# A hybrid diffusion block on one core: ScalarE evicts each time-mixer projection twice, makes the key factor and copies the decays

## The chip, the core and the metric

The kernel runs on one core of a Trainium2 chip. The metric is device time in microseconds; three timed runs of the kernel before gave 1555.4, 1558.96 and 1561.5 us. Engines are named as in the profile: PE multiplies matrices, DVE is VectorE, ACT is ScalarE, POOL is GpSimd, SP issues the transfers. Each engine runs its own instructions strictly in the order in which they stand in the program; semaphores make one wait for another.

## The reference, cut to what matters

Two layers over 1024 latent tokens and a prefix of 256 context tokens, model width 1024. The first (even) layer mixes by pooling and a short convolution. The second (odd) layer mixes by a bidirectional RWKV-7 scan over 512 channels in 8 heads, beside a Conformer convolution. The change lies in what prepares that scan:

```python
def token_shift_mix(z, mu):
    zp = jnp.pad(z, ((0, 0), (1, 1), (0, 0)))
    nb = 0.5 * (zp[:, :-2] + zp[:, 2:])
    return z + (nb - z) * mu
...
    r = token_shift_mix(r, mu[0])
    k = token_shift_mix(k, mu[1])
    v = token_shift_mix(v, mu[2])
...
    for d in range(2):
        logw = -jax.nn.softplus(-(w0[d] + jnp.tanh(uw @ w1[d]) @ w2[d])) - 0.5
        decay = jnp.exp(-jnp.exp(logw.astype(jnp.float32)))
        a = jax.nn.sigmoid(a0[d] + (ua @ a1[d]) @ a2[d])
        k_d = heads(k * (1.0 + (a - 1.0) * k_a)).astype(jnp.float32)
```

The shift is computed as (1 - mu) z + (mu / 2)(left neighbour + right neighbour): one array scaled by `omu` = 1 - mu, a sum of two neighbours, and a multiply-add with `hmu` = mu / 2. The key factor 1 + (a - 1) k_a is written with tanh: a = (1 + tanh) / 2, so that it is `ta` times one value of each channel plus another (`ka`).

## The kernel before

Channels lie on the 128 partitions, tokens along the free axis: 1024 latent tokens and 256 of the context, `TT` = 1280. The program has three parts in time: the even layer to about 609 us, the preparation of the odd layer (`odd_in`) to about 940 us, and the scan, with the Conformer branch beside it, to the end.

In `odd_in` the 512 channels are four blocks `j` of 128. For each block the job `dense` projects three arrays, keys, values and receptances (i = 0, 1, 2), with 24 matmuls for each stretch of 512 or 256 tokens (`project`, `L992`: every product of weights and activations is split into high and low parts, hence three for each of eight depths). Each stretch comes out of PSUM by a copy on ACT (`L1009`) into `Z`, an array with a column of zeros at each border. Two sets of three such arrays take turns. The weights of a projection are split by a cast on ACT (`L972`) and a subtraction on POOL (`L974`).

The job `shift` then makes the token shift: POOL adds the two neighbours into `both` (`L1061`), DVE scales `Z` in place (`L1063`) and adds the scaled `both` (`L1066`). `keys` normalises the shifted keys (`L1093` to `L1128`, on ACT, PE and DVE).

Each block then has five preparations `prep(j, u)`, one for each 256 tokens (u = 4 is the context, which comes first). One preparation, in its order of dependence: two matmuls and a tanh on ACT give `thw` (`L1149`, `L1153`); two more give `ta` (`L1160`, `L1166`); DVE adds 1 and runs two scans over `thw`, forward and backward (`L1171` to `L1173`); ACT makes the exponentials F and E of it (`L1178`, `L1180`). DVE makes the key factor `kd` from `ta` (`L1187`) and POOL multiplies it by the keys (`L1191`). DVE makes `bk` in two halves from `ta` and F (`L1194`, `L1198`, `L1199`), and the other part of it from POOL's product (`L1220`). POOL copies the decays at the ends of the 64-token chunks out of E into `PT` (`L1211`, `L1212`), multiplies receptances by E (`L1216`, into `ar`) and, for latent tokens, adds the two directions of `kd` (`L1232`, into `kb`). DVE makes the rest of `ar` (`L1223`, `L1224`) and, for latent tokens, the bonus (`L1236`, and after a matmul `L1243`). PE transposes `bk` (`L1299`), ACT and DVE copy it out of PSUM (`L1306`, `L1309`), SP stores everything. Most of these arrays (`thw`, `ta`, `E`, `F`, `kd`, `bk`, `ar`, `kb`) have one buffer each.

Four more projections (`NZ`), for the gate of the mixer, follow at the end (`L1025`, `L1027`, `L1037`).

The order of the instructions on each engine is not written out. Every job is a generator that says what it is about to issue: `yield "D", 460` is a DVE instruction with a planned cost, "A" is ACT, "G" POOL, "P" PE, "S" SP; "E" waits for a noted event, "J" for another job, "R" takes a buffer from a list (`RES2`) that `free` gives back. `Lists.run` picks the next instruction of the engine that would be free first, by priority and planned start, while the program is built; the chip then follows that order. A changed cost or engine so changes the order of the whole stage. The scan has a plan of its own.

Of the kernel before, what the change touches and what calls it, by code (L numbers as in the profile page):

```python
# [8 lines left out]
F32 = mybir.dt.float32  # L9
F32R = mybir.dt.float32r  # L10
AF = mybir.ActivationFunctionType
ALU = mybir.AluOpType
# [3 lines left out]
D = 1024  # L16
T = 1024
TC = 256
TT = T + TC
# [77 lines left out]
class Lists:  # L97
# [13 lines left out]
    def spawn(self, gen, prio):  # L111
        e = Job(gen, prio, self.cur.ready if self.cur else 0.0)
        self.advance(e)
        self.jobs.append(e)
        return e
# [6 lines left out]
    def note(self, key):  # L122
        self.ev[key] = self.cur.ready

    def free(self, name, what=None):
        self.res[name].append((self.cur.ready, what))
# [53 lines left out]
class Kern:  # L180
# [14 lines left out]
               wr=[0.0], w00=[0.0], w10=[0.0], w01=[], w11=[])  # L195
    KP = 7
    RES2 = dict(psd=[0.0] * 3, pm=[0.0], pw=[0.0] * 2, pt=[0.0], ss=[0.0], sq=[0.0], ta=[0.0], EF=[0.0], kd=[0.0], bk=[0.0], ar=[0.0],
                kb=[0.0], Vx=[0.0], X=[0.0], thw=[0.0], kkm=[0.0] * 2, ex=[0.0] * 4, LB=[0.0] * 2, gt=[0.0] * 2, wr=[], w0=[], w1=[],
                **{f"z{q}{i}": [0.0] for q in range(2) for i in range(3)})
    OP = (((0, 1), 512), ((0, 1, 4, 5, 6, 7), 0), ((4, 5, 6, 7), 512))  # L200
    NZ = 4
# [3 lines left out]
    LB = (256, 512, 0, 768)  # L205
# [678 lines left out]
    def odd_in(self, es):  # L884
        tc, nc, A = self.tc, self.nc, self.A
        cp, dr, hn = self.co, self.dr, self.hn
        hmu, omu, hw0, ka = self.hmu, self.omu, self.hw0, self.ka
# [11 lines left out]
        def rhs(src, k, b, c0, n):  # L899
            return hn[src, k, b][:, c0:c0 + n]  # L900
# [43 lines left out]
        zp = es.enter_context(tc.tile_pool(name="zp", bufs=1))  # L944

        ZS = [[zp.tile([128, TT + 3 if i < 2 else T + 2], F32, name=f"Z{q}{i}") for i in range(3)] for q in range(2)]
        for z in ZS[0] + ZS[1]:
            for c in (0, T + 1, TT + 2):
                if c < z.shape[1]:
                    nc.gpsimd.memset(z[:, c:c + 1], 0.0)  # L950
        SEG = (((1, 0, T), (T + 2, T, TC)),) * 2 + (((1, 0, T),),)

        L = Lists(self.SL, self.LAT, self.RES2)
        spawn, note, free = L.spawn, L.note, L.free
# [24 lines left out]
        def project(blocks, eat):  # L979
            i = used[0]  # L980
            used[0] += 1
            yield "E", ("w", i)
            w = self.ready[i]
            js = []
            for s, c0, m in blocks:
                yield "R", "psd"
                ps = self.psd.tile([128, 512], F32, tag="d", name="d")[:, :m]
                seq = [(k, a, b) for k in range(KD) for a, b in ((1, 0), (0, 1), (0, 0))]
                for q, (k, a, b) in enumerate(seq):
                    if q % 3 == 0:  # L990
                        yield "P", 3 * m / 2.4
                    nc.tensor.matmul(ps, lhsT=w[a][:, k, :], rhs=rhs(s, k, b, c0, m), start=(q == 0), stop=(q == len(seq) - 1))  # L992
                js.append(spawn(eat(s, c0, m, ps), 4))
            free(f"w{(n - i) % 2}")
            return js

        def dense():
            for j in range(NJ):
                spawn(keys(j), self.KP if j else 4)
                for u in (4, 0, 1, 2, 3):  # L1000
                    spawn(prep(j, u), 6 + (5 * j + (u + 1) % 5) / 100)
                spawn(over(j), 5)
                for i, blks in enumerate((BLK, BLK, XB)):
                    yield "R", f"z{j % 2}{i}"

                    def ev(src, c0, m, ps, j=j, i=i):
                        z = 1 + c0 + (0 if src == "x" else T + 1)
                        yield "A", m * 0.833 + 55
                        nc.scalar.copy(ZS[j % 2][i][:, z:z + m], ps)  # L1009
                        free("psd")  # L1010
                    spawn(shift(j, i, (yield from project(blks, ev))), self.KP if j else 4)
                    if (j, i) == (NJ - 1, 1):
                        self.s_actc.close()
                        ex = es.enter_context(tc.tile_pool(name="ex", bufs=1, side="right"))
            for i in range(self.NZ):
                yield "R", "ex"
                yield "R", "ex"
                z, g = [ex.tile([128, T], F32, tag=f"ex{i % 2}{q}", name="ex") for q in range(2)]
                spawn(gates(i, z, g, (yield from project(XB, ez(z)))), self.ZP)

        def ez(t):
            def f(src, c0, m, ps):
                z = t[:, c0:c0 + m]
                yield "A", 480
                nc.scalar.activation(out=z, in_=ps, func=AF.Tanh, scale=0.5)  # L1025
                yield "D", 605
                nc.vector.scalar_tensor_tensor(out=z, in0=z, scalar=1.0, in1=ps, op0=ALU.add, op1=ALU.mult)  # L1027
                free("psd")
            return f

        def gates(i, z, g, js):
            yield "S", 600, 3700
            nc.sync.dma_start(out=g, in_=self.GD[i])
            for e in js:
                yield "J", e
            yield "D", 1140
            nc.vector.tensor_tensor(out=z, in0=z, in1=g, op=ALU.mult)  # L1037
            yield "S", 600, 2500
            nc.sync.dma_start(out=self.ZCD[i], in_=z)
            free("ex")  # L1040
            free("ex")

        def over(j):

            for u in range(5):
                yield "E", ("prep", j, u)
            for i in range(3):
                free(f"z{j % 2}{i}")
            free("kkm")

        def shift(j, i, js):

            for e in js:
                yield "J", e
            yield "E", "room"
            yield "R", "ss"
            z, mi = ZS[j % 2][i], (1, 2, 0)[i]
            both = sp.tile([128, TT], F32, tag="ss", name="both")
            for p, o, m in SEG[i]:
                yield "G", m * 2.1 + 150  # L1060
                nc.gpsimd.tensor_tensor(out=both[:, o:o + m], in0=z[:, p - 1:p - 1 + m], in1=z[:, p + 1:p + 1 + m], op=ALU.add)  # L1061
            yield "D", 750
            nc.vector.tensor_scalar(out=z, in0=z, scalar1=omu[:, 4 * mi + j:4 * mi + j + 1], scalar2=None, op0=ALU.mult)  # L1063
            for p, o, m in SEG[i]:
                yield "D", 1.04 * m + 130
                nc.vector.scalar_tensor_tensor(out=z[:, p:p + m], in0=both[:, o:o + m], scalar=hmu[:, 4 * mi + j:4 * mi + j + 1],  # L1066
                                               in1=z[:, p:p + m], op0=ALU.mult, op1=ALU.add)
            if i:
                free("ss")
            note(("shift", j, i))  # L1070
# [4 lines left out]
        def c4(ap):  # L1075
            return ap.rearrange("p (c t) -> p c t", t=64)
# [5 lines left out]
        def folds(t):  # L1082
            return bass.AP(tensor=t.tensor, offset=t[:, 0, 1:2].offset, ap=[list(t.ap[0]), [261, 2], [65, 4], [1, 64]])
# [48 lines left out]
        def prep(j, u):  # L1132
# [6 lines left out]
            p = 1 + 256 * u + (1 if u == 4 else 0)  # L1139
            z = slice(p, p + 256)  # L1140
# [5 lines left out]
            ps = psb.tile([128, 2, 256], F32, tag="w", name="w", bufs=2)  # L1146
# [14 lines left out]
            ta = sp.tile([128, 2, 256], F32, tag="ta", name="ta")  # L1161
# [13 lines left out]
            E = sp.tile([128, 2, 261], F32, tag="E", name="E")  # L1175
# [7 lines left out]
            yield "J", jr  # L1183
            yield "R", "kd"
            kd = sp.tile([128, 2, 256], F32, tag="kd", name="kd")
            yield "D", 460
            nc.vector.tensor_scalar(out=kd, in0=ta, scalar1=ka[:, j:j + 1], scalar2=ka[:, 4 + j:5 + j], op0=ALU.mult, op1=ALU.add)  # L1187

            def scaled():
                yield "G", 1230  # L1190
# [16 lines left out]
            ar = sp.tile([128, 2, 2, 4, 64], F32, tag="ar", name="ar")  # L1207

            def ends():
                yield "G", 270  # L1210
                nc.gpsimd.tensor_copy(out=self.PT[:, j, 0, u, :], in_=E[:, 0, 64::65])  # L1211
                nc.gpsimd.tensor_copy(out=self.PT[:, j, 1, u, :], in_=E[:, 1, 1:261:65])  # L1212
                if u < 4:
                    yield "E", ("shift", j, 2)
                    yield "G", 1230
                    nc.gpsimd.tensor_tensor(out=ar[:, :, 1], in0=c4(rT[:, z]).unsqueeze(1).to_broadcast([128, 2, 4, 64]), in1=folds(E), op=ALU.mult)  # L1216
# [8 lines left out]
            js = [spawn(store_ar(j, u, ar, je), pr)]  # L1225
            yield "J", je
            free("EF")
            if u < 4:
                yield "R", "kb"
                kb = sp.tile([128, 256], F32, tag="kb", name="kb")  # L1230
# [144 lines left out]
        KK, mp, sp, thw, sm = {}, None, None, None, None  # L1375
# [4 lines left out]
        for gen, prio in ((weights(), self.WP), (stack(), 4), (gate(), 50), (room(), 5), (dense(), 100)):  # L1380
            spawn(gen, prio)
# [1017 lines left out]
```

## Time and profile before

| | us |
|---|---|
| median of three timed runs | 1558.96 |
| profiled execution, its own time | 1569.38 |
| its span, from the first to the last instruction | 1567.6 |
| mean granted TensorE clock, share of full speed | 0.938 |

| engine | busy us | share of the span |
|---|---|---|
| PE | 1393.9 | 89% |
| DVE | 1006.2 | 64% |
| ACT | 621.7 | 40% |
| POOL | 662.7 | 42% |

The span holds parts with different limits, so these shares say little of one part. What a part waits for is read from the part itself, by the busy time of each engine in that stretch, by the waits that ended there, and by the instructions in order of time. An instruction's duration in the trace includes time in which it has begun and is held up; the shortest and the median of many of one shape, beside the longest, show how much.

### The profile page before, as it was taken

Reading aid. Unit: us, or ns where it says so; the run is one execution under the profiler, and the core shown is the slowest. Engines: PE = TensorE matmul, PEld = TensorE weight load, DVE = VectorE, ACT = ScalarE, POOL = GpSimd, SP = SyncE. Lnnn points to the kernel's source line nnn. Section 1 sums busy time; section 2 is a strip of 40 time slices with the busy share of each in tenths; the row PEclk is TensorE's granted clock in tenths of the full one; section 3 lists DMA queues with packets and bytes.
Section 4 is the critical chain, followed back from the end, with each engine's and each line's share of the span. In section 5 each row is a group of like instructions: output and inputs, shape, how many; then the busy total and the mean of one; then the engine's idle time right before and its main releaser. Section 6 shows DMA issues by size and latency. Waiting matters only on the chain. (4 is left out here: it accounts for less than half of the span.)

```text
span 1567.6 us, 32131 instructions
## 1 busy us (share of the span) xinstructions
PE 1393.9 (89%) x12820; PEld 1092.7 (70%) x12820; DVE 1006.2 (64%) x1681; ACT 621.7 (40%) x1242; POOL 662.7 (42%) x925
## 2 busy tenths in 40 slices
PE   6899999999999998987988878898997988886996
PEld 1488888888888786865766656676775766674775
DVE  3746544347513732499999974878497677688567
ACT  2541111111423533445655521343454543557534
POOL 1352424252644532355565522755566246406004
PEclk9999999999999999999999989899998987878999
DMA  7413223222333112244544666655555566674233
GB/s 264 148 65 126 95 89 121 94 81 95 97 132 128 55 44 76 69 139 148 188 135 144 210 215 160 147 164 139 155 142 138 161 158 166 200 236 125 76 94 108
DMA packets 167894, 208.72 MB, mean 133 GB/s; under 512 B 38112, under 2 KB 129632, under 8 KB 167616
## 3 DMA queue, kind: packets, MB, share of 16 engines
q1 hardware_dynamic: 166448, 205.09, 43.4%
q8 instruction: 101, 1.65, 0.5%
q10 hardware_dynamic: 1296, 1.57, 0.3%
q14 instruction: 49, 0.40, 0.1%
HBM read 149.20 MB, written 55.44 MB: 131 GB/s over the span
## 5 line engine op out<-in xcount | busy, mean ns | idle before, releaser
L302 PE MATMUL d<-sx,wh 128*128 128x512 f32 x1152 | 361.6, 395 | 2.5 <-DVE sx L527 1.4
L302 PEld LDWEIGHTS d<-sx,wh 128*128 128x128 f32 x1152 | 217.2, 189 | 53.2 <-POOL sx L397 1.8
L302 PE MATMUL d<-sx,wl 128*128 128x512 f32 x576 | 229.8, 399 | 4.5 <-DVE u L822 2.7
L1396 POOL TENSOR_TENSOR tmp<-X,Bc 128x120 f32<-128x120 f32 (+2 forms) x300 | 122.1, 407 | 204.1 <-DMA Bc<-ED 181.9
L268 POOL TENSOR_TENSOR wl<-wr,wh 128x1024 fp32r<-128x1024 f32 x37 | 95.5, 2582 | 185.7 <-ACT wh L267 176.2
L992 PE MATMUL d<-sx,wh 128*128 128x512 f32 x512 | 167.5, 409 | 0.0
L1936 PE MATMUL d<-sx,wh 128*128 128x512 f32 x384 | 142.5, 439 | 0.0
L1397 POOL TENSOR_TENSOR X<-X,tmp 128x120 f32<-128x120 f32 (+2 forms) x300 | 120.1, 400 | 23.5
L302 PEld LDWEIGHTS d<-sx,wl 128*128 128x128 f32 x576 | 108.9, 189 | 29.7 <-issue 3.3
L628 DVE SCALAR_TENSOR_TENSOR junk<-wra,cb 128x1024 bf16<-128x1024 f32 x56 | 91.5, 1635 | 52.1 <-DMA wra<-in_ada_o 30.5
L992 PEld LDWEIGHTS d<-sx,wh 128*128 128x128 f32 x512 | 102.3, 200 | 23.9 <-issue 2.9
L992 PE MATMUL d<-sx,wl 128*128 128x512 f32 x256 | 116.2, 454 | 0.0
L302 PE MATMUL d<-sc,wh 128*128 128x256 f32 x576 | 104.1, 281 | 0.0
L1936 PE MATMUL d<-sx,wl 128*128 128x512 f32 x192 | 84.1, 438 | 7.4 <-DVE wl L1910 7.4
L1957 DVE SCALAR_TENSOR_TENSOR acc<-hc,vec,acc 128x960 f32<-128x960 f32 (+14 forms) x120 | 89.3, 769 | 1.1
L302 PEld LDWEIGHTS d<-sc,wh 128*128 128x128 f32 x576 | 88.8, 190 | 1.4
L1936 PEld LDWEIGHTS d<-sx,wh 128*128 128x128 f32 x384 | 75.6, 203 | 16.9 <-issue 0.2
L267 ACT CAST wh<-wr 128x1024 fp32r<-128x1024 f32 x37 | 38.7, 1045 | 117.3 <-PE d L302 86.8
L302 PE MATMUL d<-sc,wl 128*128 128x256 f32 x288 | 81.0, 281 | 0.0
L1498 PE MATMUL sc<-w,bk 64*128 64x128 f32 (+1 forms) x640 | 55.9, 313 | 21.7 <-DMA bk<-BKD 14.1
L1498 PEld LDWEIGHTS sc<-w,bk 64*128 64x128 f32 x640 | 47.0, 212 | 30.2 <-issue 24.9
L1512 DVE TENSOR_TENSOR w<-sc,cstb 64x256 f32<-64x256 f32 x80 | 33.8, 422 | 43.1 <-PE sc L1498 26.4
(380 smaller groups left out, 2909.8 us busy)
## 6 DMA issues: line engine op xcount, KB each, us to landing
wr<-in_in_o SPq DMA_DIRECT2D x32, 512.0 KB
wr<-in_in_e SPq DMA_DIRECT2D x24, 512.0 KB
wra<-in_ada_o SPq DMA_DIRECT2D x24, 512.0 KB
BKD<-bk SPq DMA_DIRECT2D x40, 256.0 KB
BTD<-X SPq DMA_DIRECT2D x20, 512.0 KB
bk<-BKD SPq DMA_DIRECT2D x40, 256.0 KB
Bc<-ED SPq DMA_DIRECT2D x20, 512.0 KB
bkt<-BTD SPq DMA_DIRECT2D x40, 256.0 KB
```

The costliest lines, as they stand in the source:

```text
L267: self.nc.scalar.copy(hi, raw)
L268: self.nc.gpsimd.tensor_tensor(out=lo, in0=raw, in1=hi.bitcast(F32), op=ALU.subtract)
L302: self.nc.tensor.matmul(ps[:, :n], lhsT=w[a][:, k, :], rhs=rhs(src, k, b, c0, n), start=(i == 0), stop=(i == len(seq) - 1))
L628: nc.vector.scalar_tensor_tensor(out=junk, in0=w, scalar=1.0, in1=cb[:, s, :], op0=ALU.mult, op1=ALU.mult, accum_out=dst[:, s:s + 1])
L992: nc.tensor.matmul(ps, lhsT=w[a][:, k, :], rhs=rhs(s, k, b, c0, m), start=(q == 0), stop=(q == len(seq) - 1))
L1396: g.tensor_tensor(out=t, in0=X[:, :, j:j + 1].to_broadcast([128, 8, m]), in1=B[:, j, :, j + 1:16] if j < 8 else B2[:, j - 8, :, j - 7:8], ...
L1397: g.tensor_tensor(out=X[:, :, j + 1:16], in0=X[:, :, j + 1:16], in1=t, op=ALU.add)
L1498: nc.tensor.matmul(ps[h][:, d, i, h:h + 1] if ctx else ps[h][:, d, i], lhsT=bk[R[h], c, d, i], rhs=w[R[h], c, d, sl, i, :], start=True, st ...
L1512: nc.vector.tensor_tensor(out=w[o, c, :, 2 * h], in0=ps[h][o, :, :, h], in1=ma[o].unsqueeze(2).to_broadcast([64, 2, 2, 64]), op=ALU.mult)
L1936: nc.tensor.matmul(ps, lhsT=wt(a, k), rhs=rhs("x", k, b, c0, 512), start=(i == 0), stop=(i == len(seq) - 1))
L1957: nc.vector.scalar_tensor_tensor(out=acc[:, o], in0=hc[:, q], scalar=w, in1=acc[:, o], op0=ALU.mult, op1=ALU.add)
```

## The change

The projections are evicted twice. A raw copy goes to a new array `zr` (two buffers, taken from `RES2` ahead of each projection), with its border columns set to zero each time, and a second reading of PSUM on ACT writes `Z` already scaled by `omu`. POOL adds the neighbours from `zr` and gives it back at once. DVE's scaling of `Z` is gone, and so are the border memsets of `Z` ahead of the stage. The key factor moves from DVE to ACT. The two POOL copies of the decays become one ACT copy with a two-step pattern.

```diff
-        for z in ZS[0] + ZS[1]:
-            for c in (0, T + 1, TT + 2):
-                if c < z.shape[1]:
-                    nc.gpsimd.memset(z[:, c:c + 1], 0.0)
...
+                    yield "R", "zr"
+                    zr = zp.tile([128, TT + 3], F32, tag="zr", name="zr", bufs=len(self.RES2["zr"]))
+                    for c in (0, T + 1, TT + 2):
+                        if c < (TT + 3 if i < 2 else T + 2):
+                            yield "G", 100
+                            nc.gpsimd.memset(zr[:, c:c + 1], 0.0)
...
                         yield "A", m * 0.833 + 55
-                        nc.scalar.copy(ZS[j % 2][i][:, z:z + m], ps)
+                        nc.scalar.copy(zr[:, z:z + m], ps)
+                        yield "A", m * 0.833 + 55
+                        nc.scalar.activation(out=ZS[j % 2][i][:, z:z + m], in_=ps, func=AF.Copy, scale=omu[:, 4 * mi + j:4 * mi + j + 1])
                         free("psd")
...
-                nc.gpsimd.tensor_tensor(out=both[:, o:o + m], in0=z[:, p - 1:p - 1 + m], in1=z[:, p + 1:p + 1 + m], op=ALU.add)
-            yield "D", 750
-            nc.vector.tensor_scalar(out=z, in0=z, scalar1=omu[:, 4 * mi + j:4 * mi + j + 1], scalar2=None, op0=ALU.mult)
+                nc.gpsimd.tensor_tensor(out=both[:, o:o + m], in0=zr[:, p - 1:p - 1 + m], in1=zr[:, p + 1:p + 1 + m], op=ALU.add)
+            free("zr")
...
-            yield "D", 460
-            nc.vector.tensor_scalar(out=kd, in0=ta, scalar1=ka[:, j:j + 1], scalar2=ka[:, 4 + j:5 + j], op0=ALU.mult, op1=ALU.add)
+            yield "A", 600
+            nc.scalar.activation(out=kd, in_=ta, func=AF.Identity, scale=ka[:, j:j + 1], bias=ka[:, 4 + j:5 + j])
...
-                yield "G", 270
-                nc.gpsimd.tensor_copy(out=self.PT[:, j, 0, u, :], in_=E[:, 0, 64::65])
-                nc.gpsimd.tensor_copy(out=self.PT[:, j, 1, u, :], in_=E[:, 1, 1:261:65])
+                yield "A", 220
+                last = E[:, 0, 64:65]
+                nc.scalar.copy(self.PT[:, j, :, u, :], bass.AP(tensor=last.tensor, offset=last.offset, ap=[list(last.ap[0]), [198, 2], [65, 4]]))
```

In the changed program line numbers differ by up to 6: the DVE part of `bk` from POOL's product is `L1225`, F is `L1183`, E `L1185`, the key factor `L1192`, POOL's product `L1196`, the decay copy `L1217`, the two evictions `L1013` and `L1015`. The stage's order is planned anew; ahead of the stage and in the scan every engine keeps its order.

On DVE, in the second preparation of the second block (j = 1, u = 0), before:

```order
L1171 TENSOR_SCALAR thw<-thw 128x2x4x64
L1172 SCALAR_TENSOR_TENSOR thw<-sm,thw 128x261
L1173 SCALAR_TENSOR_TENSOR thw<-sm,thw 128x261
L1309 COPY X<-t_5434 128x8x64
L1187 TENSOR_SCALAR kd<-ta,ka 128x512
L1194 SCALAR_TENSOR_TENSOR ta<-ta,kkm 128x512
L1198 TENSOR_TENSOR bk<-ta,F 128x4x64
L1199 TENSOR_TENSOR bk<-ta,F 128x4x64
L1220 TENSOR_TENSOR bk<-kd,F 128x8x64
L1223 SCALAR_TENSOR_TENSOR ar<-kkm,E 128x256
L1224 SCALAR_TENSOR_TENSOR ar<-kkm,E 128x4x64
```

and in the changed program:

```order
L1176 TENSOR_SCALAR thw<-thw 128x2x4x64
L1177 SCALAR_TENSOR_TENSOR thw<-sm,thw 128x261
L1178 SCALAR_TENSOR_TENSOR thw<-sm,thw 128x261
L1314 COPY X<-t_5429 128x8x64
L1199 SCALAR_TENSOR_TENSOR ta<-ta,kkm 128x512
L1203 TENSOR_TENSOR bk<-ta,F 128x4x64
L1204 TENSOR_TENSOR bk<-ta,F 128x4x64
L1225 TENSOR_TENSOR bk<-kd,F 128x8x64
L1228 SCALAR_TENSOR_TENSOR ar<-kkm,E 128x256
L1229 SCALAR_TENSOR_TENSOR ar<-kkm,E 128x4x64
```

The row of the key factor is gone from DVE and nothing else changed places.

On ACT, in the same preparation, before, from F on:

```order
L1178 ACTIVATE F<-thw 128x522
L1180 ACTIVATE E<-thw 128x522
L1153 ACTIVATE thw<-w,hw_88 128x4x64 x2
L1009 COPY Z_4362<-d 128x512
L1262 COPY Vx<-m 128x256
L1204 COPY bk<-bk 64x8x64
L1166 ACTIVATE ta<-w,hw_88 128x256 x2
```

and in the changed program:

```order
L1183 ACTIVATE F<-thw 128x522
L1185 ACTIVATE E<-thw 128x522
L1192 ACTIVATE kd<-ta,ka 128x512
L1013 COPY zr<-d 128x512
L1015 ACTIVATE Z_4362<-d,omu 128x512
L1158 ACTIVATE thw<-w,hw_88 128x4x64 x2
L1267 COPY Vx<-m 128x256
L1209 COPY bk<-bk 64x8x64
L1217 COPY PT<-E 128x2x4
L1171 ACTIVATE ta<-w,hw_88 128x256 x2
```

The key factor stands behind both exponentials, the eviction has become two, and the decay copy has come in. In 12 of the 20 preparations one to four further instructions stand between F and the key factor. The longest such piece, in the third preparation of the first block of the changed program:

```order
L1183 ACTIVATE F<-thw 128x522
L1013 COPY zr<-d 128x256
L1015 ACTIVATE Z_4365<-d,omu 128x256
L1185 ACTIVATE E<-thw 128x522
L1267 COPY Vx<-m 128x256
L968 CAST wh<-wr 128x1024
L1192 ACTIVATE kd<-ta,ka 128x512
```

There a double eviction, a copy of values and the cast of a weight are ahead of it.

## Rows read from the trace of the kernel before

**Rows 1.** Busy time in the stretch: length, PE, PEld, DVE, ACT, POOL, clock, DMA.
```profile
660.00:927.00 267.00, 224.21 (x1266) 178.10 (x1265) 252.35 (x318) 136.85 (x247) 150.53 (x122) 0.94 0.53 164
```

**Rows 2.** Waits from 660 to 927 us: total us, times, longest.
```profile
DVE ex L1027 <- ACT ex L1025: 2.7, 2, 2.1
...
ACT Z L1009 <- PE d L992: 22.2, 10, 6.3
...
PE m L1241 <- DVE kb L1236: 15.8, 7, 4.1
...
POOL kd L1191 <- DVE kd L1187: 71.0, 20, 6.5
```

**Rows 3.** Groups of the removed instructions: busy us, mean ns, idle before.
```profile
L1063 DVE TENSOR_SCALAR Z<-Z,omu 128x1283 f32<-128x1283 f32 x8 | 10.5, 1306 | 7.3 <-POOL both L1061 7.3
...
L1063 DVE TENSOR_SCALAR Z<-Z,omu 128x1026 f32<-128x1026 f32 x4 | 3.8, 948 | 0.0
...
L1187 DVE TENSOR_SCALAR kd<-ta,ka 128x512 f32<-128x512 f32 x20 | 13.2, 659 | 1.1 <-ACT ta L1166 1.1
...
L1211 POOL COPY PT<-E 128x4 f32<-128x4 f32 x20 | 11.4, 572 | 0.0
...
L1212 POOL COPY PT<-E 128x4 f32<-128x4 f32 x20 | 7.8, 388 | 0.0
...
L950 POOL MEMSET Z<- 128x1 f32 x16 | 0.6, 107 | 0.0
```

**Rows 4.** Shortest, median and longest ns of a line; first and last start.
```profile
L1063 DVE TENSOR_SCALAR Z<-Z,omu x12: 723/876/2995, 641.4 to 875.2; 128x1283 f32<-128x1283 f32 x8, 128x1026 f32<-128x1026 f32 x4
...
L1173 DVE TENSOR_TENSOR_SCAN thw<-sm,thw x20: 667/675/2820, 670.7 to 914.0; 128x261 f32<-128x261 f32 x20
...
L1187 DVE TENSOR_SCALAR kd<-ta,ka x20: 514/537/2035, 673.4 to 918.5; 128x512 f32<-128x512 f32 x20
...
L1191 POOL TENSOR_TENSOR kd<-kd,Z x20: 1089/1534/1597, 674.0 to 919.2; 128x512 f32<-128x512 f32 x20
...
L1211 POOL COPY PT<-E x20: 183/386/1183, 675.5 to 920.2; 128x4 f32<-128x4 f32 x20
```

**Rows 5.** DVE in order of time, one preparation (j = 1, u = 0): start, us.
```profile
745.01 0.41 DVE L1171 TENSOR_SCALAR thw<-thw 128x512 f32<-128x512 f32 x1
...
746.08 0.67 DVE L1173 TENSOR_TENSOR_SCAN thw<-sm,thw 128x261 f32<-128x261 f32 x1
...
747.25 0.54 DVE L1187 TENSOR_SCALAR kd<-ta,ka 128x512 f32<-128x512 f32 x1
...
750.01 0.68 DVE L1220 TENSOR_TENSOR bk<-kd,F 128x512 f32<-128x512 f32 x1
750.61 1.41 DVE L1223 SCALAR_TENSOR_TENSOR ar<-kkm,E 128x256 f32<-128x256 f32 x1
...
752.83 2.11 DVE L1171 TENSOR_SCALAR thw<-thw 128x512 f32<-128x512 f32 x1
```

**Rows 6.** POOL in order of time, same place.
```profile
747.94 1.53 POOL L1191 TENSOR_TENSOR kd<-kd,Z 128x512 f32<-128x512 f32 x1 [4.41 <-DVE kd L1187]
...
750.09 1.65 POOL L1216 TENSOR_TENSOR ar<-Z,E 128x512 f32<-128x512 f32 x1
```

**Rows 7.** ACT in order of time, same place.
```profile
747.05 0.64 ACT L1178 ACTIVATE F<-thw 128x522 f32<-128x522 f32 x1
747.59 0.63 ACT L1180 ACTIVATE E<-thw 128x522 f32<-128x522 f32 x1
```

**Rows 8.** ACT prices: evictions, and a short copy without and with an operand per partition.
```profile
L1009 ACT COPY Z<-d 128x512 f32<-128x512 f32 x24 | 14.0, 583 | 30.9 <-PE d L992 30.9
...
L1009 ACT COPY Z<-d 128x256 f32<-128x256 f32 x8 | 3.0, 370 | 2.8 <-PE d L992 2.8
...
L1596 ACT COPY x<-PI x20: 244/266/268, 990.0 to 1450.0; 128x128 f32<-128x128 f32 x20
...
L1584 ACT ACTIVATE Xe<-X,cstb x40: 384/387/402, 988.0 to 1446.6; 128x128 f32<-128x128 f32 x40
```

More of the change, by code (lines that the diff above doesn't have):

```diff
@@ L197 @@
     RES2 = dict(psd=[0.0] * 3, pm=[0.0], pw=[0.0] * 2, pt=[0.0], ss=[0.0], sq=[0.0], ta=[0.0], EF=[0.0], kd=[0.0], bk=[0.0], ar=[0.0],
-                kb=[0.0], Vx=[0.0], X=[0.0], thw=[0.0], kkm=[0.0] * 2, ex=[0.0] * 4, LB=[0.0] * 2, gt=[0.0] * 2, wr=[], w0=[], w1=[],
+                kb=[0.0], Vx=[0.0], X=[0.0], thw=[0.0], kkm=[0.0] * 2, ex=[0.0] * 4, LB=[0.0] * 2, zr=[0.0] * 2, gt=[0.0] * 2, wr=[], w0=[], w1=[],
                 **{f"z{q}{i}": [0.0] for q in range(2) for i in range(3)})
@@ L1004, in dense, with ev @@
                     yield "R", f"z{j % 2}{i}"
-                    def ev(src, c0, m, ps, j=j, i=i):
+                    yield "R", "zr"
[4 more added lines that the diff above has]
+                            nc.gpsimd.memset(zr[:, c:c + 1], 0.0)
+                    def ev(src, c0, m, ps, j=j, i=i, zr=zr):
+                        mi = (1, 2, 0)[i]
                         z = 1 + c0 + (0 if src == "x" else T + 1)
                         yield "A", m * 0.833 + 55
-                        nc.scalar.copy(ZS[j % 2][i][:, z:z + m], ps)
+                        nc.scalar.copy(zr[:, z:z + m], ps)
+                        yield "A", m * 0.833 + 55
+                        nc.scalar.activation(out=ZS[j % 2][i][:, z:z + m], in_=ps, func=AF.Copy, scale=omu[:, 4 * mi + j:4 * mi + j + 1])
                         free("psd")
-                    spawn(shift(j, i, (yield from project(blks, ev))), self.KP if j else 4)
+                    spawn(shift(j, i, zr, (yield from project(blks, ev))), self.KP if j else 4)
                     if (j, i) == (NJ - 1, 1):
@@ L1049, in over, with shift @@
             free("kkm")
-        def shift(j, i, js):
+        def shift(j, i, zr, js):
             for e in js:
```

## The prediction, made before the changed kernel had run

> **What bounds the kernel now.** I read the stretches first, then the waits inside the one that the change touches, then the groups of the moved instructions, and last the order of time in one preparation. The moved work lies in the time-mixer stage, and nearly all of it between 660 and 927 us. There DVE is busy 252.35 of 267 us, ACT 136.85, POOL 150.53 and PE 224.21 [rows 1]. DVE's longest wait in the whole stretch adds up to 2.7 us, while POOL waits 71.0 us for DVE's `kd` alone, ACT 22.2 us for projections, and PE 15.8 us for DVE's `kb` [rows 2]. So here DVE is the engine that sets the pace and the others stand waiting for it. The rest of the program (even layer, scan) keeps its order of instructions on every engine, so a gain in this stage moves the scan forward unchanged.
>
> DVE's busy time is not all its own. One of its scans takes 0.667 us at the shortest and 2.82 us at the longest, with the same shape; the scale of a projection goes from 0.723 to 2.995 us and the key factor from 0.514 to 2.035 us [rows 4]. In order of time one sees why: DVE's `L1223` took 1.41 us from 750.61 while POOL's `L1216` ran 1.65 us from 750.09, and DVE came free just after POOL did [rows 5, 6]. DVE and POOL hold each other up.
>
> The Trainium skill, page "SBUF — State Buffer", section "Who interferes with whom", states that a DVE instruction with two SBUF inputs, or in a two-port mode, and a GpSimd instruction that reads SBUF exclude each other for a whole instruction. The trace agrees, with those 1.41 and 1.65 us. By that rule only the own time of a removed DVE instruction is gained, since the wait passes to the next DVE instruction: 20.2 us of the 27.5 below; without it all 27.5.
>
> **The change part by part.** The sum is made for the profiled execution, 1569.38 us, which is 10.4 us above the median of 1558.96 us; the difference is carried over to the median.
>
> *Scaling of the projections leaves DVE.* Eight of 1.306 us and four of 0.948 us, 14.3 us together [rows 3]. Their own time goes by the shortest and the median of `L1063`, 0.723 for the four narrow and 0.876 for the eight wide ones [rows 4]: 8 x 0.876 + 4 x 0.723 = 9.9 us. What was waiting for POOL will wait in the next instruction, so I take -9.9, bounds -14.3 and 0.
>
> *The key factor leaves DVE.* 20 of 0.659 us are 13.2 us [rows 3], own time 20 x 0.514 = 10.3 us [rows 4]. I take -10.3, bounds -13.2 and 0; but it adds a wait. Before, `L1187` was issued as soon as DVE had finished the scans, POOL began `L1191` at 747.94, 1.19 us after the end of the last scan (746.08 + 0.67), and DVE began `L1220` at 750.01, 3.26 us after it [rows 5, 6]. Now kd stands on ACT behind F and E, which also wait for the scans. F and E start 0.54 us apart [rows 7], so kd starts some 1.1 us after the scans. Its duration is bounded below by F's 0.64 us, nearly the same size without a per-partition operand [rows 7], and above by two such operands at the difference of `L1584` and `L1596`, 0.387 - 0.266 = 0.12 us each [rows 8]: 0.64 to 0.88, taken as 0.8. POOL's product starts at about 2.0 and takes 1.09 us at the shortest and 1.53 at the median [rows 4]. So DVE can start its `L1225` 3.1 to 3.5 us after the scans, where without `L1187` it would be there at 3.26 - 0.54 = 2.7. At this place the removed 0.54 us comes back as a wait of 0.4 to 0.8 us. In 16 of 20 preparations the two `kb` instructions also stand on DVE ahead of it and hide more. Bounds 0 to 20 x 0.8 = 16; I take 20 x 0.3 = +6. Queued behind the waiting `L1225` on DVE are the two `ar` products and the next scans, for which F and E of the next preparation wait.
>
> *Something else ahead of kd on ACT.* In 12 of the 20 preparations the new ACT order has one to four further instructions between F and kd (evictions, weight casts, parts of the key normalisation). Priced between a narrow copy of 0.370 us [rows 8] for 12, 4.4 us, and two wide scaled evictions of 0.7 us for each of 12, 17 us. DVE mostly has key or shift work at those places that covers it. Bounds 0 to 17, taken +4.
>
> The Trainium skill, page "ScalarE: Activation LUTs", section "What ACT_TABLE_LOAD costs", gives 186 ns + 0.833 ns per element and 93 ns per pointer operand. By it kd would be an estimated 0.80 us; the trace's difference for one operand is 0.12 us rather than 0.093, and the sum is the same by either.
>
> *Double evictions.* The raw copy stays as it was; the scaled one is new: 24 x (0.583 + 0.12) + 8 x (0.370 + 0.12) = 20.8 us of ACT [rows 8]. With kd (20 x 0.8 = 16) and the decay copies (20 at `L1596`'s 0.27 = 5.3), ACT gains 42 us, about 179 busy of some 254 us. It has the room. A PSUM buffer comes free 0.7 us later, but three are there and PE is not the pace. Cost 0, hidden by DVE's work; bounds 0 and +20.8 if the cover were gone.
>
> *Decay copies leave POOL.* 20 of 0.572 and 20 of 0.388 us, 19.2 us [rows 3], own time 40 x 0.183 = 7.3 us [rows 4]. POOL is not the pace, but while it copies DVE can be held up, and the `ar` product behind the copies starts earlier. Bounds -7.3 and 0; I take -3.
>
> *Borders.* 16 small memsets become 32, at 0.107 us [rows 3]: at most +1.7 us on an engine with waits; 0.
>
> Sum: -9.9 - 10.3 + 6 + 4 - 3 = -13.2 us, so 1569.4 becomes 1556 and the median 1558.96 becomes 1546.
>
> **The rivals.** (1) *All own time returns.* DVE and POOL exclude each other, and the stretch is nearly full with the two; then every own microsecond off either counts: -20.2 - 7.3 = -27.5, 1531.5 us. The 252 of 267 us busy speak for it, the kd chain against. PE's 224 us of busy time would still fit in 267 - 27.5 = 239.5, so PE is no floor before that. That is also what the SBUF page's rule gives if it is the only limit; the trace's 1.41 us wait bears it out as a mechanism, not as the only one.
>
> (2) *No change.* The recurrence scans, F, E, kd, POOL's product, `L1225`, `ar`, next scans sets the period, which was 752.83 - 745.01 = 7.8 us in a preparation without fillers [rows 5]. If the waits take the upper bound of 16 and the ACT neighbours 7, the -20.2 - 3 is used up: about 1559. The place computed above speaks for it, the fillers in 16 of 20 against.
>
> (3) *Slower.* ACT becomes the link that comes last. ACT waited 22.2 us for projections in its row, up to then at no cost to kd [rows 2]; now a kd behind such a wait, or behind a doubled eviction, stops POOL and DVE. If ACT's added 42 us stood on the path against 20.2 + 7.3 + 3 us given back, the result is about +12, 1571 us. It decides once the delay is above 30.5 / 20 = 1.5 us for each preparation. In 12 preparations there is something ahead of kd; but few reach 1.5 us, and ACT has 30% of idle time.
>
> **How the numbers follow.** Forecast (-8 to -20) 0.50; rival 1 0.17; rival 2 0.22; rival 3 0.11. 0.5% is 7.8 us, about what a measurement of this kernel can tell from no change: faster 0.67, within it 0.22, slower 0.11. The likeliest case alone gives 1539 to 1551. The range goes down to rival 1's 1531 and up to 1563, which leaves out most of rival 3 and of the bounds beyond rival 1.
>
> **What would show it.** In the profile after: the stage's end, where DVE starts the scan's first weights, comes 10 to 20 us earlier; no DVE scale or key factor; DVE's busy share of the stage falls below 94%, with new waits of `L1225` for POOL's kd of 5 to 15 us in sum; POOL waits for ACT instead of DVE; kd on ACT at 0.75 to 0.9 us, scaled evictions at about 0.7 us; ACT near 70% busy. It is wrong if `L1225` waits under 3 us (rival 1), or if DVE's waits for ACT and POOL pass 25 us (rivals 2 and 3), or if PE's projections end the stage.

## The result, and the profile after

The changed kernel took 1574.32 us (median), the kernel before 1559.91 us beside it: ratio 1.0087, 95% interval 1.0062 to 1.0112. It is slower; 1546 us were forecast. The profile shown here is of a second series of executions of the same kernel (median 1575.92 us, ratio 1.0077, 1.0029 to 1.0125), since the profiled execution of the first was a slow one of 1625.06 us at a granted clock of 0.817.

Its profiled execution took 1569.41 us, no longer than that of before. The part from the scan's first weights on, which the change leaves alone, lasted 622 us here and 631 us there; over the other profiles of this study, too, it lies between 622 and 632 us. So profiles are compared by the stage, and kernels by their timed ratios.

The stretch of [rows 1], in the kernel after:

```profile
660.00:927.00 267.00, 221.68 (x1211) 173.13 (x1210) 229.14 (x274) 163.06 (x306) 128.52 (x103) 0.92 0.53 155
```

DVE is busy 229.14 us instead of 252.35, and POOL 128.52 instead of 150.53: the work left as planned. But 1211 of PE's matmuls fall into the stretch, where 1266 did: the stage goes slower with less to do. Its waits, which answer to [rows 2]:

```profile
POOL kd L1196 <- ACT kd L1192: 89.8, 18, 7.7
...
ACT zr L1013 <- PE d L988: 16.9, 10, 4.2
...
DVE ta L1199 <- ACT kd L1192: 12.5, 10, 2.6
DVE kb L1248 <- PE m L1246: 11.5, 8, 3.3
PE m L1246 <- DVE kb L1241: 10.4, 8, 1.9
...
DVE ss L1122 <- ACT sq L1120: 5.9, 3, 2.2
...
DVE ss L1103 <- PE ks L1111: 1.4, 2, 0.9
...
DVE X L1314 <- PE t L1304: 0.7, 1, 0.7
```

Before, no wait of DVE came to more than 2.7 us in sum. Now its longest is at `L1199`, for ACT's key factor, and its second for a matmul. `L1225`, where I had put the new wait, is not among them. Shortest, median and longest of single lines, as in [rows 4]:

```profile
L1178 DVE TENSOR_TENSOR_SCAN thw<-sm,thw x20: 668/675/2829, 669.8 to 924.4; 128x261 f32<-128x261 f32 x20
...
L1192 ACT ACTIVATE kd<-ta,ka x20: 797/803/826, 671.6 to 927.2; 128x512 f32<-128x512 f32 x20
...
L1196 POOL TENSOR_TENSOR kd<-kd,Z x20: 1088/1598/1696, 672.5 to 928.1; 128x512 f32<-128x512 f32 x20
...
L1217 ACT COPY PT<-E x20: 194/203/208, 675.4 to 932.6; 128x8 f32<-128x8 f32 x20
```

The starts of the second scan measure the stage: first to last of the 20 preparations, 669.8 to 924.4, is 254.6 us; before it was 670.7 to 914.0, 243.3 us [rows 4]. These 11.3 us are most of the loss, which the two ratios put at 12.0 and 13.6 us. Now the preparation of [rows 5] in order of time, DVE:

```profile
746.86 0.41 DVE L1176 TENSOR_SCALAR thw<-thw 128x512 f32<-128x512 f32 x1
...
747.92 0.68 DVE L1178 TENSOR_TENSOR_SCAN thw<-sm,thw 128x261 f32<-128x261 f32 x1
748.52 0.67 DVE L1314 COPY X<-t 128x512 f32<-128x512 f32 x1
750.60 0.69 DVE L1199 SCALAR_TENSOR_TENSOR ta<-ta,kkm 128x512 f32<-128x512 f32 x1 [1.42 <-ACT kd L1192]
751.38 1.14 DVE L1203 TENSOR_TENSOR bk<-ta,F 128x256 f32<-128x256 f32 x1
752.45 1.41 DVE L1204 TENSOR_TENSOR bk<-ta,F 128x256 f32<-128x256 f32 x1
753.78 1.22 DVE L1225 TENSOR_TENSOR bk<-kd,F 128x512 f32<-128x512 f32 x1
...
755.60 0.42 DVE L1176 TENSOR_SCALAR thw<-thw 128x512 f32<-128x512 f32 x1
```

POOL, as in [rows 6]:

```profile
750.65 1.60 POOL L1196 TENSOR_TENSOR kd<-kd,Z 128x512 f32<-128x512 f32 x1 [5.61 <-ACT kd L1192]
752.21 1.37 POOL L1221 TENSOR_TENSOR ar<-Z,E 128x512 f32<-128x512 f32 x1
```

and ACT, as in [rows 7]:

```profile
748.69 0.66 ACT L1183 ACTIVATE F<-thw 128x522 f32<-128x522 f32 x1
749.23 0.64 ACT L1185 ACTIVATE E<-thw 128x522 f32<-128x522 f32 x1
749.76 0.81 ACT L1192 ACTIVATE kd<-ta,ka 128x512 f32<-128x512 f32 x1
```

The scans end at 748.60. The key factor starts 1.16 us later and POOL's product 2.05 us later: 1.1 and 2.0 were forecast. But DVE stands before `L1199` until that same moment. `L1199` writes `ta` in place, and ACT must have read it. The period is 755.60 - 746.86 = 8.74 us, before 7.82: the wait of 1.42 less the removed 0.54 us is 0.88 of the 0.92. Afterwards DVE's short products run beside POOL and are held up (1.41 us for `L1204`, which took 0.41 in the preparation just ahead): in this preparation that is no new loss, since before it was `L1223` that took 1.41.

### The profile page after: what moved, and what is told of

It is laid out like the page before. It is cut to its first block, busy times and chain, and to the rows that moved or that the text cites. A ratio compares the mean times of both kernels' runs of the same rounds, so it can differ in the third digit from the quotient of the medians.

```text
span 1623.1 us, 32158 instructions
## 1 busy us (share of the span) xinstructions
PE 1473.8 (91%) x12820; PEld 1116.1 (69%) x12820; DVE 984.2 (61%) x1649; ACT 654.6 (40%) x1314; POOL 645.2 (40%) x901
## 4 chain that ended last, share of the span: by engine, by line
PE 57%; DVE 15%; DMA 9%; POOL 7%; ACT 6%; issue 5%; SPq 1%; DVEq 0%; ACTq 0%; POOLq 0%
PE d L302 31%; PE d L988 5%; DMA Bc<-ED 4%; PE d L1941 4%; PE d L2083 3%; POOL X L1402 3%; POOL tmp L1401 3%; PE sc L1503 2%; PE d L920 2%; DMA bk<-BKD 1%; PE pr L457 1%; PE pa L1727 1%; PE d L2288 1%; DMA ad<-in_ada_e 1%; DVE bk L1204 1%
## 5 line engine op out<-in xcount | busy, mean ns | idle before, releaser
L302 PE MATMUL d<-sx,wh 128*128 128x512 f32 x1152 | 386.7, 419 | 2.3 <-DVE sx L527 1.4
L302 PEld LDWEIGHTS d<-sx,wh 128*128 128x128 f32 x1152 | 222.5, 193 | 69.5 <-DVE sx L527 1.7
L302 PE MATMUL d<-sx,wl 128*128 128x512 f32 x576 | 243.3, 422 | 1.8 <-DVE u L822 1.4
L988 PE MATMUL d<-sx,wh 128*128 128x512 f32 x512 | 177.3, 431 | 0.0
L1941 PE MATMUL d<-sx,wh 128*128 128x512 f32 x384 | 147.4, 452 | 0.0
L988 PEld LDWEIGHTS d<-sx,wh 128*128 128x128 f32 x512 | 103.8, 203 | 29.7 <-issue 3.0
L988 PE MATMUL d<-sx,wl 128*128 128x512 f32 x256 | 120.3, 470 | 0.0
L628 DVE SCALAR_TENSOR_TENSOR junk<-wra,cb 128x1024 bf16<-128x1024 f32 x56 | 86.4, 1542 | 53.7 <-DMA wra<-in_ada_o 30.8
L302 PE MATMUL d<-sc,wh 128*128 128x256 f32 x576 | 109.7, 291 | 0.0
L1941 PE MATMUL d<-sx,wl 128*128 128x512 f32 x192 | 87.4, 455 | 7.9 <-DVE wl L1915 7.9
L302 PEld LDWEIGHTS d<-sc,wh 128*128 128x128 f32 x576 | 92.7, 196 | 2.0
L1941 PEld LDWEIGHTS d<-sx,wh 128*128 128x128 f32 x384 | 75.9, 204 | 19.1 <-issue 0.2
L1196 POOL TENSOR_TENSOR kd<-kd,Z 128x512 f32<-128x512 f32 x20 | 30.7, 1537 | 94.2 <-ACT kd L1192 88.2
```

Source lines behind the costliest of these rows:

```text
L302: self.nc.tensor.matmul(ps[:, :n], lhsT=w[a][:, k, :], rhs=rhs(src, k, b, c0, n), start=(i == 0), stop=(i == len(seq) - 1))
L628: nc.vector.scalar_tensor_tensor(out=junk, in0=w, scalar=1.0, in1=cb[:, s, :], op0=ALU.mult, op1=ALU.mult, accum_out=dst[:, s:s + 1])
L1941: nc.tensor.matmul(ps, lhsT=wt(a, k), rhs=rhs("x", k, b, c0, 512), start=(i == 0), stop=(i == len(seq) - 1))
```

## The experiments

Three theories stood at the start. A: the key factor on ACT costs, by the stop at `L1199` (first form) or by POOL's late product and what waits for it (second form). B: ACT's load, above all the doubled evictions, costs. C: the stage's new order costs. "Planned anew" means that the planner sees the new engine and cost and orders the whole stage by them. "Held plan" below means that the instruction is issued on the other engine while the planner still sees the old engine and cost, so that DVE and PE keep their order. The stretch is that between the first and the last start of the second scan, as above; ratios are to the kernel before.

| kernel | ratio | 95% interval | stretch, us |
|---|---|---|---|
| changed kernel again | 1.0077 | 1.0029 to 1.0125 | 254.6 |
| key factor alone | 1.0072 | 1.0050 to 1.0095 | 256.4 |
| evictions alone | 0.9924 | 0.9899 to 0.9949 | 231.0 |
| decay copies alone | 0.9977 | 0.9948 to 1.0006 | 242.0 |
| evictions and decay copies | 1.0011 | 0.9981 to 1.0040 | 248.1 |
| changed, product in its own array | 1.0056 | 1.0029 to 1.0082 | 250.0 |
| changed, key factor early | 1.0063 | 1.0038 to 1.0089 | 247.6 |
| key factor alone, held plan | 1.0102 | 1.0063 to 1.0140 | 262.5 |
| evictions, decay copies, held plan | 0.9943 | 0.9915 to 0.9971 | 231.8 |
| whole change, held plan | 1.0045 | 1.0018 to 1.0072 | 249.5 |
| changed, own array first, key factor behind | 1.0010 | 0.9988 to 1.0033 | 245.0 |
| the same, decay copies on POOL | 1.0059 | 1.0027 to 1.0091 | 253.0 |
| held plan, product in its own array | 0.9969 | 0.9946 to 0.9993 | 237.5 |
| held plan, key factor early | 0.9942 | 0.9915 to 0.9968 | 232.9 |

**The parts by themselves.** First the changed kernel again, then the kernel before with one part each (the hunks of the change as shown above).

> The changed kernel once more, for a profile at the ordinary clock. Theory A (key factor): DVE's in-place product L1199 overwrites ta, which ACT's key factor still has to read, so DVE stops there until ACT has made F, E and kd; with POOL's product, which starts at the same moment and holds the port, that costs about 1.1 us for each of 20 preparations. It expects 14 us slower than before, L1199 waiting for kd 10 to 15 us in sum, and the whole loss inside the stage from 609 us to the scan's start. Theory B (ACT load): the second eviction of 0.7 us stands ahead of what DVE and PE wait for; it expects the added DVE waits to be mainly for PE and for ACT instructions other than kd. Theory C (a new plan, and the two raw buffers that limit how far the projections run ahead): waits spread, with PE starved at the raw buffers.

> The kernel before with the key factor alone moved to ACT, planned anew. A: slower than before by 10 to 20 us, L1199's counterpart waits for kd 8 to 15 us. B: within 4 us of before. C: some few us either way.

> The changed kernel with the key factor back on DVE and the decay copies back on POOL: double eviction and raw buffers alone. A: faster than before by 5 to 12 us, since DVE has 12 instructions (14.3 us with waits, 9.9 us of their own) less. B and C: slower than before by 8 to 15 us.

> The kernel before with the decay copies alone moved to ACT, planned anew. A: 0 to 5 us faster. B: within 2 us. C: some few us either way, which would show what a new plan alone can do.

The changed kernel again waits at `L1199` as A had it. But between the first and the last scan that is 12.5 of the 25.0 us that all of DVE's waits for ACT and PE have grown by (8.3 before, 33.3 now); the other half are waits for PE and for other work of ACT, so B has its share there. The evictions alone gain 0.76%, the decay copies at most a little, and the key factor alone loses 0.72%, nearly the whole loss. By the forecasts A holds in all three, and B falls for the evictions. But the three ratios multiply to 0.9972, not 1.0077: the parts don't add.

**Without the key factor.** The changed kernel with the key factor back on DVE:

```diff
-            yield "A", 600
-            nc.scalar.activation(out=kd, in_=ta, func=AF.Identity, ...)
+            yield "D", 460
+            nc.vector.tensor_scalar(out=kd, in0=ta, ...)
```

> The changed kernel with the key factor alone put back on DVE: double eviction, raw buffers and the decay copy on ACT stay. A (the key factor on ACT costs, the rest gains): about 12 to 17 us faster than before, the sum of the two parts measured alone (-11.9 and -4.3). B (ACT's load is what costs, so parts add up badly on it): less than 8 us faster.

Evictions and decay copies together gain nothing, though each part gains or is neutral: here A's forecast fails and B's holds. Still, without the key factor's move the changed kernel is 0.66% or some 10 us faster (1.0011 against 1.0077), much as the key factor alone would have it. The longest waits of its DVE, from 660 to 930 us:

```profile
DVE kb L1248 <- PE m L1246: 8.7, 7, 2.3
...
DVE sq L1126 <- ACT sq L1124: 5.5, 4, 1.4
...
DVE X L1314 <- PE t L1304: 4.2, 5, 1.4
DVE ss L1103 <- PE ks L1111: 3.7, 3, 1.8
```

The waits for PE are what grew: 16.6 us here, 4.3 with the evictions alone, while those for ACT are 12.9 and 11.6. It can be the ACT copy or the order that came with it.

**That order held.** The kernel with the evictions alone, the decay copies issued on ACT at the old plan:

```diff
                 yield "G", 270
-                nc.gpsimd.tensor_copy(...)
+                nc.scalar.copy(self.PT[:, j, :, u, :], ...)
```

> Evictions doubled on ACT, the key factor on DVE, the decay copies issued on ACT in the same places of a plan that is held: DVE and PE have the very order of the kernel with the evictions alone (0.992 of before). Theory C (the new plan of the stage lost what the decay copies and evictions gain together, 1.001 for the two): about 0.990 to 0.993, some 1551 us, and the first-to-last-scan stretch stays at 234 us. Theory B (the added ACT work itself delays the chain): about 1.000, 1562 us, with DVE's waits for ACT grown.

The gain is back: 0.9943 against 1.0011, intervals apart. So an order cost some 10 us (0.0068 x 1562), and not the copy on ACT as such.

**The key factor at a held plan.** On top of the last kernel, and also on the kernel before:

```diff
             yield "D", 460
-            nc.vector.tensor_scalar(out=kd, in0=ta, ...)
+            nc.scalar.activation(out=kd, in_=ta, func=AF.Identity, ...)
```

> The whole change, but with the plan held at that of the kernel with the evictions alone: the key factor and the decay copies are issued on ACT where that plan has them on DVE and POOL. Theory A (the key factor on ACT costs through the stop at the in-place product and POOL's late start): slower than before, about 1.004 to 1.010, since the evictions' gain of 12 us is taken back by 20 stops of about 1.5 us; DVE waits for ACT's kd at L1199 20 to 30 us. Theory C (the plan costs): 0.985 to 0.993.

> The kernel before with the key factor on ACT, but planned as if it still were DVE's 460 ns, so that all other instructions keep their order. A: still slower than before, by 5 to 12 us, with L1194's counterpart waiting for kd. C (the new plan is what cost in only_kd): within 4 us of before or faster.

Both lose 1.0%: 1.0045 / 0.9943 = 1.0103, and 1.0102. That is 16 us for this one instruction (10 to 22 by the second's interval), with the order of all else unchanged; C's forecasts fail, and the second loses more than A's 5 to 12 us. The second has single evictions, so they are not needed for the loss. Here the trace counts it. Without the move (decay copies and evictions on ACT at the held plan), DVE's second scan and some of DVE's waits for PE and ACT:

```profile
L1178 DVE TENSOR_TENSOR_SCAN thw<-sm,thw x20: 669/674/1041, 672.4 to 904.2; 128x261 f32<-128x261 f32 x20
```

```profile
DVE ss L1122 <- ACT sq L1120: 3.9, 2, 2.3
...
DVE kb L1248 <- PE m L1246: 1.7, 5, 0.8
...
DVE ss L1103 <- PE ks L1111: 0.6, 1, 0.6
...
DVE X L1314 <- PE t L1304: 0.3, 1, 0.3
```

With it:

```profile
L1178 DVE TENSOR_TENSOR_SCAN thw<-sm,thw x20: 668/675/2781, 670.8 to 920.3; 128x261 f32<-128x261 f32 x20
```

```profile
DVE ta L1199 <- ACT kd L1192: 28.3, 18, 3.5
```

and in the kernel before with the key factor on ACT:

```profile
DVE ta L1194 <- ACT kd L1187: 30.2, 18, 3.2
```

The stretch grows from 231.8 to 249.5 us, by 17.7. The new wait of 28.3 us less the removed own time of 20 x 0.514 = 10.3 us is 18.0. That these agree so closely is in part luck, as the whole count of the stretch shows (length, PE, PEld, DVE, ACT, POOL, clock, DMA; first without, then with the move):

```profile
672.40:904.20 231.80, 201.50 (x1156) 159.19 (x1154) 219.03 (x285) 143.04 (x274) 121.92 (x96) 0.95 0.59 175
```

```profile
670.80:920.30 249.50, 208.67 (x1165) 164.14 (x1163) 212.34 (x265) 155.57 (x293) 123.55 (x96) 0.92 0.56 163
```

DVE's busy time falls by 6.7 us and not by 10.3, and all its waits in the stretch grow from 10.6 to 35.8 us, by 25.2. The granted clock falls as well, but DVE's waits for PE do not grow with it (2.8 and 2.2 us), so a slower PE is not seen to hold DVE up here.

**Taking the stop away.** In the changed kernel, once with the product in an array of its own, once with the key factor made right behind the tanh that gives `ta`, in one of two buffers; the edit of the first:

```diff
-            nc.vector.scalar_tensor_tensor(out=ta, in0=ta, ...)
+            tb = sp.tile([128, 2, 256], F32, tag="tb", name="tb")
+            nc.vector.scalar_tensor_tensor(out=tb, in0=ta, ...)
```

> The changed kernel, but DVE's product L1199 writes a tile of its own and no longer overwrites ta, so it need not wait until ACT has read ta for the key factor. A1 (the stop at L1199 is the cost): the wait for kd goes and 8 us or more of the 13 come back. A2 (the cost is that POOL's product starts late and then collides with DVE's products and the next scans; where DVE stops does not matter): under 5 us come back, and DVE waits at L1225's counterpart or is held up longer by POOL instead.

> The changed kernel, but ACT makes the key factor right after the tanh ta, ahead of F and E (two kd buffers), so that POOL's product need not wait for the scans. A1 and A2: the wait of L1199 for kd goes nearly to 0, and the time comes to about no_kd's, 12 us or more faster than before, since 20 x 0.51 us of DVE work is gone too. B: ACT carries the same load, so it stays slower than before by 8 us or more.

Both move little, within the intervals of the changed kernel: the first as A2 had it, the second as B had it. But both were planned anew. `kb` waits for PE's matmul 15.3 us in the first (8.7 without the key factor's move). Two more were planned anew with the own array issued ahead of the key factor, the second with the decay copies on POOL:

> The changed kernel with the product of L1199 in an array of its own, issued before the key factor, which is a job of its own on ACT planned at 800 ns, beside POOL's product. Theory A in its first form (the stop at the in-place product is the loss): no such stop is left, so the forecast gain comes out, 0.990 to 0.995. Theory A in its second form (POOL's late product, and what waits for it, carries the loss): still 1.000 to 1.006, with neither DVE nor POOL at work for 25 us or more between the first and the last scan.

> As the run before, with the decay copies left on POOL. If the ACT copy of the decays is what makes evictions and decay copies together gain nothing (theory B): 5 to 10 us faster than the run before. If only the plan matters (theory C): either sign, within 6 us of it. If the key factor on ACT costs whatever it waits for (A, second form): slower than the evictions alone (0.992) by 8 to 14 us, about 1.000.

1.0010 and 1.0059: the first is the ratio that A's second form forecast, the second fits none of its three. The second is the slower though it has less on ACT, so its loss against the first is not ACT's. Between kernels that are planned anew, half a per cent says nothing of the part that was changed. So the same two remedies at the held plan:

> The whole change at the held plan (1.0045, against 0.9943 with the key factor on DVE), with the product of L1199 in an array of its own, so that DVE need not wait there for ACT's reading of ta. If the stop at L1199 (28 us in sum) is the whole loss: 0.985 to 0.992, the first-to-last-scan stretch at 224 to 232 us. If POOL's product, which starts 2.0 us after the scans behind F, E and kd, carries it: the waits move on to the instruction that needs the product, 0.997 to 1.004, the stretch at 243 to 252 us. Half of each: 0.993 to 0.997.

> The whole change at the held plan, with the key factor made on ACT right behind the tanh that gives ta, ahead of the scans, in one of two buffers; so neither DVE's product in place nor POOL's product waits for F and E. If the place behind F and E is the loss (either form of A): 0.982 to 0.990, better than any kernel so far, with waits at L1199 under 3 us. If 0.8 us more on ACT ahead of F costs by itself (B): 0.995 to 1.005, with DVE or POOL waiting for ACT's ta, F or thw.

With its own array the ratio falls from 1.0045 to 0.9969: the stop is some three quarters of the 1.03%, by the intervals anything from 0.4% up. The longest waits of that kernel's DVE (lines one higher from `L1199` on):

```profile
DVE bk L1226 <- POOL kd L1196: 6.6, 5, 1.8
DVE kb L1249 <- PE m L1247: 6.2, 11, 1.9
...
DVE ss L1122 <- ACT sq L1120: 5.3, 3, 2.8
```

Only where the product has an array of its own does the wait appear that I had forecast, DVE's part of `bk` for POOL's product: here at 6.6 us (+6 was taken), and at 2.8 us or less in the kernels planned anew. With the key factor early this goes too (0.9942), yet the kernel is no faster than with the key factor on DVE (0.9943), and neither forecast, A's 0.982 to 0.990 nor B's 0.995 to 1.005, is met. Its waits (lines two higher from `L1199` on):

```profile
DVE kb L1250 <- PE m L1248: 8.6, 10, 2.6
...
DVE ss L1122 <- ACT sq L1120: 4.8, 2, 2.6
...
DVE X L1316 <- PE t L1306: 2.5, 3, 0.9
...
DVE ss L1103 <- PE ks L1111: 2.1, 4, 1.0
```

These four sum to 18.0 us; in the kernel with the key factor on DVE the same four sum to 6.5. Counted over all lines between the first and the last scan, DVE's waits for PE grow from 2.8 to 11.1 us and those for ACT from 6.3 to 9.5, again 11.5 together. That is what the key factor's 10.3 us became. Either DVE comes earlier and meets PE's chain, or ACT, with 16 us more in its queue, makes PE and DVE late. No run takes the key factor off DVE without giving it to ACT, so the two are not told apart.

Of all kernels the one with the evictions alone is the fastest, 0.9924 (0.9899 to 0.9949), 1551.29 us; the two at 0.994 can't be told from it.

## Why the prediction was wrong

The step that failed is the key factor's: forecast at -0.3 us, it measured +16 us at a held order. What the runs showed in its place is a stop of DVE at `L1199`, 28.3 us in sum. The evictions' term held, and the decay copies' can't be told from its forecast.

- *The engine that sets the pace, and durations:* right for the kernel before, as the evictions' gain shows. Key factor 0.803 us (0.8 taken), wide scaled evictions 0.70 (0.7), start of the key factor and of POOL's product within 0.1 us in the preparation shown.
- *Scaling off DVE, -9.9:* right. Alone 0.0076 x 1562 = -11.9 us, interval -15.8 to -8.0.
- *Decay copies, -3:* alone -3.6, and +3 on top of the evictions at the held plan (0.9943 / 0.9924); neither can be told from zero.
- *Key factor, -10.3 with +6 and +4 of waits:* this step failed. I asked when DVE could start `L1225`, three instructions behind, and let the `kb` work ahead of it hide the wait. I named as queued behind it only `ar` and the next scans. That `L1199` overwrites the key factor's input, and stands first, I did not see; on one engine the order kept the two apart at no cost. At the held plan the wait at `L1199` alone is 28.3 us instead of 10 in all, so the step is +16 (1.0103) instead of -0.3. Where the stop is taken away, the forecast wait is there with 6.6 us, but even so the step comes to +4 (0.9969 / 0.9943), since DVE's waits for PE grow too.
- *"A gain on DVE moves the stage":* true for the evictions, not for the second 10 us. With neither stop nor late product, 11.5 us of new waits for PE and ACT eat the 10.3. I had excluded PE by its busy time (224 us would fit in 239.5), but the chain goes through PE and back to DVE (`kb`, matmul, `L1248`), and a busy total doesn't bound that. How much of it is ACT's added load is open.
- *The plan:* I priced parts as if each kept the others' place. The steps are, by the ratios: evictions -11.9, decay copies +3.0, key factor +16, and the order of the changed kernel against the held plan +5.0 (1.0077 / 1.0045; its intervals don't exclude zero). The sum is +12.1 us, 0.77% of 1562. It must come out so, since the steps are quotients of neighbouring ratios; it is no further evidence.
- *Rival 3* (1571 us) had the size, in part by luck: it decides above 1.5 us for each preparation, and the stop is 28.3 / 20 = 1.4 at the held plan and 12.5 / 20 = 0.6 in the changed kernel. That a late key factor on ACT stops DVE and POOL was its mechanism; its reason, a wait or an eviction ahead of the key factor, is not needed: in the preparation shown none is there, and the kernel with single evictions loses as much.
- *What would show it:* `L1225` without a wait would have read as rival 1; the stop ahead of it hid it. DVE's waits for ACT and POOL were to pass 25 us. In the changed kernel those at `L1199` and `L1122` are 18.4, beside 13.6 for PE, so this sign stayed away from a kernel that is slower; at the held plan the one at `L1199` is 28.3 alone. ACT was to be near 70% busy; it is 163.06 of 267 us, 61%.

Open is which exchange in the new order costs the 10 us of evictions with decay copies. The traces show DVE's waits for PE there, and PE in turn waits longer for ACT's copies of the values, from 660 to 930 us, in the new order and in the held one:

```profile
PE m L1263 <- ACT Vx L1267: 14.4, 6, 4.7
```

```profile
PE m L1263 <- ACT Vx L1267: 6.0, 7, 1.6
```

TensorE's granted clock between the first and the last scan is 0.92 there, against 0.95 in the held order (means over the stretch). Whether it is a consequence of these waits or adds to the loss is not shown, and no run isolates one exchange.

## What to carry to other kernels

Before an operation goes to another engine, list who overwrites what it reads: an in-place update that was free on one engine becomes a wait at the head of the other queue, and whatever stands behind it is late too. Where a planner sets the order, try a move once with the old plan held and once planned anew; the first tells what the move costs in that order, and here the second differed by up to 10 us, as much as the gains sought. An engine's saved time counts only until something else comes last: here no order that was tried gained more than some 12 us.

## What was unexpected of the hardware

One ACT copy of 128 x 8 elements in a two-step pattern took 0.203 us (0.27 taken), where the two POOL copies took 0.572 and 0.388 on average. POOL's product, which starts beside `L1199` in most preparations, took 1.60 us at the median and 1.09 at the shortest.
